# One decoder layer on one core: the output projection in a written TensorE order, logit constants by one product, and shortened hops in the routing chain

## The chip, the cores and the metric

The kernel runs on one core of a Trainium2 chip. A core has a matrix engine (TensorE; PE in the profile, its weight loads PEld), a vector engine (DVE), a scalar engine (ACT), a fourth engine (GpSimd; POOL) and a fifth that mostly issues DMAs (SyncE; SP). Each runs its own list of instructions in order; they wait for one another by semaphores. The metric is the device time of one execution in microseconds, less being better. Three executions of the kernel before took 1434.85, 1434.45 and 1433.2 us, with a median of 1434.45 us.

## The reference

One decoder layer on x of 1024 rows by 1024 columns, in float32. What matters here is its second half:

```python
# o: the merged result of two attention branches, 1024x1024
h = layer_norm(ALPHA * x + o @ w_out, ln1_g, ln1_b)
g_logits = h @ w_grp + b_grp             # 4 groups
g_sel = argmax(g_logits)                 # one group for each row
e_logits = (h @ w_rtr + b_rtr)[g_sel]    # 8 experts in that group
top_l, top_i = top_k(e_logits, 2)
weight = softmax(g_logits)[g_sel] * softmax(top_l)
# each row goes to its two experts of 32:
# y = (silu(h @ w_gate[e]) * (h @ w_up[e])) @ w_down[e]
out = layer_norm(ALPHA * h + sum(weight * y), ln2_g, ln2_b)
```

## The kernel before

The program has these stages, one after another: the input projections, the two attention branches, the merge of the branches (products of L711), the output projection with layer norm and routing, the 32 experts, and the last layer norm. The change touches the output projection, the routing and the first experts; the lists of all engines are the same up to there.

**Output projection.** The 1024 rows are worked in 8 tiles of 128 rows (the loop over `i`). A tile is 48 products of 128x512 (L982): 8 slices `k` of the inner dimension, three terms each (high by high, high by low and low by high halves of split operands), and two halves of the columns. The last tile does all products of its first half before those of its second. DVE then drains the sum into `wr` (L985, with ALPHA·x added), takes mean and variance (L987, L792, L794, with a power on POOL, L795) and applies the layer norm in two operations: L799 (minus the mean, times the gain) and L800 (times 1/deviation, plus the bias). TensorE transposes the normalised rows (L490, 8 squares), ACT copies them to `hT` (L1001), and 8 products `hT` by `wrt` (L956, two instructions each) give 36 router logits for each row; DVE adds the router bias `brt` (L963). SP writes the rows to `h_d` (which the experts gather from) and to `acc_d` (which they add to).

**Constants of this stage.** `gb1` (gain and bias of the layer norm, L828 and L829), `wrt` (router weights, L831), `brt` (L833) and `cons` (a table of small constants, L835) are loaded by SP, in this order. `prefetch` (L752) loads expert weights of 1 MB each into a ring of slots as these come free; SP issues these on the same queue.

**Routing.** `route` works a group of tiles at once, groups (0,1), (2,3,4), (5,6) and (7). DVE finds the best group and the two best experts (`first_max`, L858 to L865), makes the 0/1 matrix `am` (L888) and running counts `ac` (L898); TensorE turns these into places (`pp`, L899 and L900); DVE builds `at_place` (L922) and TensorE turns values into lists for each expert (`ft`, L923). The last group ends with `tkv` (L926, L927), the rows and weights of each expert. POOL scatters the same into `tab` (`store`, L938); the last groups' scatters (`late`) stand after the first gathers. Then experts that got over 128 rows are counted (L1017 to L1031, `novi`).

**Experts.** For each expert POOL gathers its rows from `h_d` (L1049, needs `tkv` and the written `h_d`), TensorE transposes them (`turn`, L1066), ACT and DVE split them (L59, L60) and the weights (`parts`, L1076, L1077) into high and low halves, TensorE multiplies (`up` L1089, `down` L1112), and POOL adds the result to `acc_d` (L1117). An expert's 3 MB of weights free their slots as they are split, and the next loads start from that.

**What sets the order.** Tiles of shared memory come from pools with few buffers (`s` three, `pt` one, `pv` one). In the output projection a scheduler that simulates the program places the instructions of all engines; `tc.issue_after` holds single pieces back. In the experts the order of TensorE is that of the code.

## Time and profile before

| what | value |
| --- | --- |
| median of three runs | 1434.45 us |
| profiled execution | 1431.84 us |
| its span | 1430.1 us |
| TensorE busy | 1331.9 us, 93% of the span |
| DVE busy | 1114.9 us, 78% |
| ACT busy | 764.4 us, 53% |
| POOL busy | 460.3 us, 32% |
| mean granted TensorE clock | 0.968 of full speed |

The profiled execution has 1.7 us outside of its span, and it is 2.6 us below the median of the three runs. Times in the rows are microseconds from the start of the span. TensorE is busy nearly everywhere, so the places that matter are those where it is not: in 40 slices of 36 us each, only the slice from 1037 us on (6 tenths) and the last two are below 8 tenths. The output projection runs from 921 us to 1030 us, the routing of the last tiles up to 1048 us, and the experts from 1053 us to 1387 us.

### The profile page before, as it was taken

How to read it: one execution, taken by the hardware profiler on the slowest of the kernel's cores; microseconds unless marked ns; L12 is line 12 of the kernel's file. 1: busy time of each engine (PE TensorE's matmuls, PEld its weight loads, DVE VectorE, ACT ScalarE, POOL GpSimd, SP SyncE). 2: the span in 40 equal slices, each digit the busy share in tenths (PEclk: the TensorE clock that was granted, in tenths of full speed). 3: DMA queues.
4: the chain of work that ended last, by engine and by line, in shares of the span. 5: the costliest groups of instructions: out<-in, count | busy, mean ns of one | idle time of the engine just before them, and what ended most of it. 6: DMA issues, size and time to landing. Idle time of an engine off the chain costs nothing. (4 is left out here: it accounts for less than half of the span.)

```text
span 1430.1 us, 20066 instructions
## 1 busy us (share of the span) xinstructions
PE 1331.9 (93%) x6779; PEld 1100.2 (77%) x6795; DVE 1114.9 (78%) x2273; ACT 764.4 (53%) x1378; POOL 460.3 (32%) x463
## 2 busy tenths in 40 slices
PE   8999999999999999999999999999969999998960
PEld 7878888878887787888878778888757778776640
DVE  5323699889997787888889965655869999998856
ACT  4323323221116788888879731211238888886744
POOL 1112323222223335453444100001334454443326
PEclk9999999999998999999999999999969999999985
DMA  6023334498333232732521264664659999999936
GB/s 234 16 74 133 111 116 149 152 279 285 138 106 112 67 107 90 195 105 82 152 74 38 97 264 160 253 237 154 230 186 329 344 325 317 317 329 329 320 74 235
DMA packets 69477, 261.36 MB, mean 183 GB/s; under 512 B 15092, under 2 KB 16974, under 8 KB 57085
## 3 DMA queue, kind: packets, MB, share of 16 engines
q1 hardware_dynamic: 59644, 243.24, 49.3%
q0 software_dynamic: 9728, 16.82, 5.1%
q8 instruction: 54, 0.88, 0.3%
q14 instruction: 51, 0.41, 0.1%
HBM read 219.19 MB, written 70.70 MB: 203 GB/s over the span
## 5 line engine op out<-in xcount | busy, mean ns | idle before, releaser
L1089 PE MATMUL pt<-slot,slot 128*128 128x512 f32 x768 | 199.9, 407 | 10.3 <-DVE slot L1077 4.9
L1077 DVE TENSOR_TENSOR slot<-slot,slot 128x1024 fp32r<-128x1024 f32 x160 | 191.3, 1219 | 15.8 <-ACT slot L1076 11.7
L1076 ACT CAST slot<-slot 128x1024 fp32r<-128x1024 f32 x160 | 165.8, 1048 | 36.9 <-PE pt L1089 25.9
L1089 PEld LDWEIGHTS pt<-slot,slot 128*128 128x128 f32 x768 | 142.1, 192 | 49.7 <-DVE slot L1077 8.9
L186 POOL TENSOR_TENSOR wl<-wr,wh 128x1024 fp32r<-128x1024 f32 x39 | 94.9, 2434 | 264.5 <-ACT wh L185 256.0
L324 DVE TENSOR_SCALAR_CACHE_REDUCE jk<-idx,cand 128x384 bf16<-128x384 f32 (+1 forms) x186 | 164.4, 942 | 1.2
L60 DVE TENSOR_TENSOR ptl<-pt,pth 128x512 fp32r<-128x512 f32 (+1 forms) x240 | 148.5, 638 | 18.5 <-ACT pth L59 17.5
L204 PE MATMUL s<-xh,wh 128*128 128x512 f32 x496 | 154.9, 393 | 2.4 <-DVE wi L168 1.4
L204 PE MATMUL s<-xh,wl 128*128 128x512 f32 x496 | 154.5, 391 | 0.0
L204 PE MATMUL s<-xl,wh 128*128 128x512 f32 x496 | 154.4, 391 | 0.0
L59 ACT CAST pth<-pt 128x512 fp32r<-128x512 f32 (+1 forms) x240 | 127.8, 548 | 45.4 <-PE pt L490 38.6
L465 POOL TENSOR_SCALAR pb<-pb,st 128x128 f32<-128x128 f32 (+3 forms) x120 | 91.7, 783 | 183.1 <-ACT pth L59 55.5
L185 ACT CAST wh<-wr 128x1024 fp32r<-128x1024 f32 x39 | 41.0, 1051 | 190.9 <-PE s L204 92.2
L1117 POOL DMA_INDIRECT acc_d<-wr,tkv x32 | 76.8, 2400 | 138.7 <-DVE wr L1116 132.5
L204 PEld LDWEIGHTS s<-xh,wh 128*128 128x128 f32 x496 | 92.5, 188 | 22.9 <-issue 2.6
L204 PEld LDWEIGHTS s<-xl,wh 128*128 128x128 f32 x496 | 93.6, 189 | 19.5
L204 PEld LDWEIGHTS s<-xh,wl 128*128 128x128 f32 x496 | 93.4, 189 | 19.3
L484 ACT ACTIVATE pb<-pb,st 128x128 f32<-128x128 f32 (+7 forms) x128 | 99.6, 779 | 15.5 <-DVE st L482 14.4
L1112 PE MATMUL s<-slot,hT 128*128 128x512 f32 x384 | 100.7, 408 | 2.0 <-DVE hT L60 1.5
L982 PE MATMUL s<-slot,slot 128*128 128x512 f32 x384 | 93.5, 398 | 0.0
L1112 PEld LDWEIGHTS s<-slot,hT 128*128 128x128 f32 x384 | 70.6, 191 | 26.8 <-DVE hT L60 11.2
L490 PE MATMUL pt<-ident,pb 128*128 128x128 f32 x576 | 90.5, 276 | 0.7 <-DVE ptl L60 0.4
(340 smaller groups left out, 2918.8 us busy)
## 6 DMA issues: line engine op xcount, KB each, us to landing
slot<-in_w_ex_dram SPq DMA_DIRECT2D x80, 1024.0 KB
wr<-in_w_tt_dram SPq DMA_DIRECT2D x31, 512.0 KB
ring<-in_w_ex_dram SPq DMA_DIRECT2D x11, 1024.0 KB
b_d<-r_d SPq DMA_DIRECT2D x16, 576.0 KB
xw<-in_xw_dram SPq DMA_DIRECT2D x8, 718.0 KB
last<-in_w_ex_dram SPq DMA_DIRECT2D x5, 1024.0 KB
z_ga<-sh SPq DMA_DIRECT2D x8, 512.0 KB
slot<-b_d SPq DMA_DIRECT2D x8, 512.0 KB
```

The lines of the kernel that those rows point to most:

```text
L59: S.copy(h, src)
L60: V.tensor_tensor(l, src, f(h), op=ALU.subtract)
L186: G.tensor_tensor(wl, wr, f(wh), op=ALU.subtract)
L204: PE.matmul(z[:, c], w[:, k * P:(k + 1) * P], xx[:, k, c], start=(k == 0 and w is wh and xx is xh), stop=(k == KD - 1 and w is wl))
L324: V.tensor_scalar(jk[:, :n], idx[:, OFF[i]:OFF[i] + n], t, None, op0=op, op1=ALU.add, accum_out=cnt[:, i - 2:i - 1])
L465: G.tensor_scalar(ap, ap, s, 1.0, op0=ALU.mult, op1=ALU.mult)
L484: S.activation(p, p, AF.Exp, bias=st[:, 0, j:j + 1], scale=-1.0, accum_out=st[:, 1, j:j + 1])
L982: mm = PE.matmul(s[:, HALF[c]], MS[i][:, a, k], WO[k][:, b, HALF[c]], start=(k == 0 and x == 0), stop=(k == KD - 1 and x == 2)).ins
L1076: S.copy(w[:, 0], self.w[k2 // 4][:, k2 % 4 // 2])
L1077: d = V.tensor_tensor(w[:, 1], self.w[k2 // 4][:, k2 % 4 // 2], f(w[:, 0]), op=ALU.subtract).ins
L1089: PE.matmul(self.a, self.xt[:, a, k * P:(k + 1) * P], w[:, b, (k - k2) * 512:(k - k2 + 1) * 512], start=(k == 0 and x == 0), stop=(k == KD ...
L1112: PE.matmul(s[:, c], self.hT[:, a, k * P:(k + 1) * P], w[:, b, c], start=(k == 0 and x == 0), stop=(k == 1 and x == 2))
```

## The change

**Order of the output projection.** The scheduler no longer places TensorE's instructions there. The products are a generator that stops after each slice `k`, and a table (`hook`) says what stands between: transposes of the tile before, its logits, and pieces of the routing. The other engines are still placed by the scheduler.

**Logits.** The rows are transposed before the layer norm. The gain is multiplied into `wrt` once, and a logit is then (1/deviation) · (row · (gain·W) − mean · sum(gain·W)) + (sum(bias·W) + router bias). The two sums (`nu` and `vb`) come from DVE products and sums over `wrt` and `cons` (which now also holds gain and bias, in 16 more columns) and from one product of TensorE with a matrix of ones (`logit_constants`, L944), which stands in tile 0 behind 7 of its 8 slices. The router bias is loaded behind `cons`, into `vb`.

**Routing.** The groups are (0,1), (2,3), (4,5), (6) and (7); `route` is a generator in three pieces (up to the counts, up to `at_place`, the rest), and the pieces of the earlier groups are called from the table. In the last chain products that nobody uses (`keep_warm`, 14, 4 and 16 of 128x512) stand between the hops.

**The last tile.** The layer norm's second operation on it (`shift`) is issued in two halves: one after its logits, one after the first piece of its routing; the write to `h_d` follows. Its first half is transposed and multiplied with the router before the products of its second half are all done.

**First experts.** Expert 0's rows are split in two halves and its products go in another order of terms. The count of overfull experts (18 small operations of DVE) moves behind expert 0's split, and the load of `novi` on SP moves behind four weight loads. The scatters of groups (4,5), (6) and (7) into `tab` (8 instead of 2) stand behind expert 3's gather on POOL. The descriptor memory goes from 8192 to 4096.

```diff
+            for x in HALF if self.n == 0 else (slice(0, T),):
+                self.split = split(self.xt[:, 0, x], self.xt[:, 1, x], s[:, x])
...
+            terms = list(enumerate(((0, 0), (1, 0), (0, 1)) if self.n else ((0, 0), (0, 1), (1, 0))))
+            for k, (x, (a, b)) in ([(k, t) for t in terms for k in (k2, k2 + 1)] if self.n == 0 else
+                                   [(k, t) for k in (k2, k2 + 1) for t in terms]):
...
-        brt = wo.tile([P, 36], F32, name="brt")
-        nc.sync.dma_start(brt, A["b_rt"].partition_broadcast(P))
-        cons = wo.tile([P, 328], F32, name="cons")
+        cons = wo.tile([P, 344], F32, name="cons")
         nc.sync.dma_start(cons, A["cons"])
+
+        nu, vb = wo.tile([P, 36], F32, name="nu"), wo.tile([P, 36], F32, name="vb")
+        nc.sync.dma_start(vb, A["b_rt"].partition_broadcast(P))
+        ones_f, gsum = wo.tile([P, P], F32, name="ones_f"), wo.tile([P, 2, 36], F32, name="gsum")
+        bw = wo.tile([P, KD, 36], F32, name="bw")
+        G.memset(ones_f, 1.0)
+        V.tensor_tensor(bw, wrt, cons[:, 336:344, None].to_broadcast([P, KD, 36]), op=ALU.mult)
+        V.tensor_tensor(wrt, wrt, cons[:, 328:336, None].to_broadcast([P, KD, 36]), op=ALU.mult)
+        for x, w in enumerate((wrt, bw)):
+            V.tensor_reduce(gsum[:, x], w.rearrange("p k e -> p e k"), axis=X, op=ALU.add)
+
+        def logit_constants():
+            t = ps.tile([P, 512], F32, name="pv")
+            PE.matmul(t[:, 0:72], ones_f, gsum.rearrange("p x e -> p (x e)"), start=True, stop=True)
+            V.tensor_scalar(nu, t[:, 0:36], -1.0, None, op0=ALU.mult)
+            V.tensor_tensor(vb, vb, t[:, 36:72], op=ALU.add)
...
+            for j in range(B):
+                d = V.tensor_tensor(ac[:, i0 + j + 1], ac[:, i0 + j], am[:, j], op=ALU.add).ins
+            yield d
             pp = ps.tile([P, 512], F32, name="pv")[:, 0:32 * B].rearrange("p (b e) -> p b e", b=B)
             for j in range(B):
-                V.tensor_tensor(ac[:, i0 + j + 1], ac[:, i0 + j], am[:, j], op=ALU.add)
                 PE.matmul(pp[:, j], tri, am[:, j], start=True, stop=False)
                 PE.matmul(pp[:, j], ones_b[:, 0:P], ac[:, i0 + j], start=False, stop=True)
...
+            at_places = []
+            for j in range(B):
+                for x in range(2):
+                    at_places.append(wo2.tile([P, P], F32, name="at_place", bufs=4))
+                    V.tensor_scalar(at_places[-1], places, sf[:, 0, j, x:x + 1], None, op0=ALU.is_equal)
+            yield
...
-            if i0 + B < NT:
+            if i0 + B < 5:
...
-            if last:
-                with tc.issue_after(mm):
-                    logits(hT, lt, range(KD))
-                held = gather(i - 1, lt)
...
-                    done = scale(xr[:, cc], gb1[:, :, cc], mv, rs)
...
-            if i != NT - 2:
-                logits(hT, lt, range(KD))
-            nc.sync.dma_start(h_d[ts], xr)
-            kept.append(nc.sync.dma_start(acc_d[ts], xr).ins)
-            if last:
-                with tc.issue_after(done):
-                    route(*held)
-            if i != NT - 2:
-                g = gather(i, lt)
-                if g:
-                    route(*g)
...
+        GROUPS = {1: (0, 2), 3: (2, 2), 5: (4, 2), 6: (6, 1), 7: (7, 1)}
...
+        def turn_rows(i, c):
+            if c == 0:
+                hT = wo2.tile([P, T], F32, name="hT", bufs=1)
+                rows[i] += (hT, ps.tile([P, 512], F32, name="pt"))
+            xr, hT = rows[i][0], rows[i][2]
+            t = transposed([xr[:, k * P:(k + 1) * P] for k in range(4 * c, 4 * c + 4)])
+            S.copy(hT[:, HALF[c]], t)
...
+            V.scalar_tensor_tensor(xr, xr, mv[:, 0:1], gb1[:, 0], op0=ALU.subtract, op1=ALU.mult)
+            if i < NT - 1:
+                shift(i, slice(0, D))
+
+        def shift(i, cc):
+            xr, ts, rs = rows[i][0], slice(i * P, (i + 1) * P), rows[i][5]
+            V.scalar_tensor_tensor(xr[:, cc], xr[:, cc], rs, gb1[:, 1, cc], op0=ALU.mult, op1=ALU.add)
+            if cc.stop == D:
+                nc.sync.dma_start(h_d[ts], xr)
+                kept.append(nc.sync.dma_start(acc_d[ts], xr).ins)
...
+            o = lgs[e][:, i - i0]
+            V.scalar_tensor_tensor(o, nu, mv[:, 0:1], lt[:, 0:36], op0=ALU.mult, op1=ALU.add)
+            d = V.scalar_tensor_tensor(o, o, rs, vb, op0=ALU.mult, op1=ALU.add).ins
+            if i == NT - 1:
+                with tc.issue_after(d):
+                    shift(i, HALF[0])
+            if i == e:
+                routes[e] = route(i0, lgs[e], B)
+                d = next(routes[e])
+            if i == NT - 1:
+                with tc.issue_after(d):
+                    shift(i, HALF[1])
...
+        def hook(i, at):
+            if i == NT - 1:
+                at = {3: (0, 1), 7: (2,), 9: (3,), 11: (5,), 12: (4,), 14: (6,)}.get(at, ())
+            else:
+                at = {0: (7,), 1: (0, 1), 3: (2,), 5: (3,)}.get(at, ())
+            for x in at:
+                if x < 2 and i > 0:
+                    turn_rows(i - 1, x)
+                    if x:
+                        norm(i - 1)
+                elif x == 2 and i > 0:
+                    logits(i - 1, 0)
+                    logits(i - 1, 1)
+                elif x in (3, 4) and i - 2 in routes:
+                    next(routes[i - 2])
+                elif x == 7 and i - 3 in routes:
+                    next(routes[i - 3])
+                elif x == 5:
+                    turn_rows(i, 0)
+                elif x == 6:
+                    logits(i, 0)
...
+        def keep_warm(n):
+            t = ps.tile([P, 512], F32, name="s")
+            for x in range(n):
+                PE.matmul(t, ident_b, ones_b[:, 0:512], start=(x == 0), stop=(x == n - 1))
+        with tc.manual_schedule(engines={mybir.EngineType.PE}):
+            for i in range(NT):
+                for at, _ in enumerate(products(i)):
+                    hook(i, at)
+                    if i == 0 and at == 6:
+                        logit_constants()
+                prefetch({0: 6, 2: 1, 4: 1, 6: 1, 7: 5}.get(i, 0))
+            last = NT - 1
+            next(routes[6])
+            turn_rows(last, 1)
+            norm(last)
+            logits(last, 1)
+            next(routes[6])
+            keep_warm(14)
+            next(routes[7])
+            keep_warm(4)
+            next(routes[7])
+            ex = {e: make(e) for e in range(2)}
+            for e in range(2):
+                ex[e].fetch()
+            overflow = ps.tile([P, 512], F32, name="pv")[:, 0:32]
+            PE.matmul(overflow, ones_b[:, 0:P], ac[:, NT], start=True, stop=True)
+            keep_warm(16)
...
+    def count_overflow():
...
+        V.tensor_copy(novi, novf)
...
-    with tc.issue_after(ex[1].fetched):
-        late[0]()
...
+            if e == 2:
+                with tc.issue_after(ex[3].fetched):
+                    for store in late:
+                        store()
+            with tc.issue_after(last_place[0]) if e == 0 else nullcontext():
+                ex[e].up(0)
+                ex[e].up(2)
+                if e > 0:
+                    ex[e - 1].flip()
+                if e == 0:
+                    with tc.issue_after(ex[0].split):
+                        count_overflow()
...
-    nc = bacc.Bacc("TRN2", target_bir_lowering=False, num_devices=1, dynamic_dma_scratch_size=8192)
+    nc = bacc.Bacc("TRN2", target_bir_lowering=False, num_devices=1, dynamic_dma_scratch_size=4096)
```

TensorE at the end of tile 0, before. `slot_9420` to `slot_9455` are the split output weights of the 8 slices, `slot_8976` and `slot_9479` the split rows of tiles 0 and 1.

```order
L982 MATMUL s<-slot_9440,slot_8976 128x512 x6
L982 MATMUL s<-slot_9445,slot_8976 128x512 x6
L982 MATMUL s<-slot_9450,slot_8976 128x512 x6
L982 MATMUL s<-slot_9455,slot_8976 128x512 x6
L982 MATMUL s<-slot_9420,slot_9479 128x512 x6
L982 MATMUL s<-slot_9425,slot_9479 128x512 x6
```

The same place now (L1087 is the product that was L982).

```order
L1087 MATMUL s<-slot_9440,slot_8976 128x512 x6
L1087 MATMUL s<-slot_9445,slot_8976 128x512 x6
L1087 MATMUL s<-slot_9450,slot_8976 128x512 x6
L944 MATMUL pv<-gsum,ones_f 128x72
L1087 MATMUL s<-slot_9455,slot_8976 128x512 x6
L1087 MATMUL s<-slot_9420,slot_9493 128x512 x6
L1087 MATMUL s<-slot_9425,slot_9493 128x512 x6
L490 MATMUL pt<-ident,wr 128x128 x8
```

The product of the constants stands between the seventh and the eighth slice of tile 0, and tile 0's transposes follow two slices into tile 1.

DVE around tile 0, before: the split of tile 1's rows, the drain of tile 0 (L985) and its layer norm.

```order
L60 TENSOR_TENSOR slot_9479<-slot_8863,slot_9479 128x1024
L985 SCALAR_TENSOR_TENSOR wr<-wr,s 128x1024
L60 TENSOR_TENSOR slot_9581<-slot_8864,slot_9581 128x1024
L987 BN_STATS bs<-wr 128x6 x2
L792 BN_AGGR mv<-bs 128x2
L794 TENSOR_SCALAR rs<-mv 128x1
L799 SCALAR_TENSOR_TENSOR wr<-wr,mv,gb_9458 128x1024
L800 SCALAR_TENSOR_TENSOR wr<-wr,rs,gb_9458 128x1024
L838 CAST tri<-cons 128x128
L841 CAST vali<-cons 128x8 x2
```

The same stretch now: what makes `gsum` (L937 to L940, with casts of other constants between) and what reads the constants' product stands ahead of the drain (L1092).

```order
L60 TENSOR_TENSOR slot_9493<-slot_8863,slot_9493 128x1024
L937 TENSOR_TENSOR bw<-wrt,cons 128x288
L950 CAST tri<-cons 128x128
L953 CAST vali<-cons 128x8 x2
L1200 COPY pid<-cons 128x1
L938 TENSOR_TENSOR wrt<-wrt,cons 128x288
L940 TENSOR_REDUCE gsum<-bw 128x36
L940 TENSOR_REDUCE gsum<-wrt 128x36
L945 TENSOR_SCALAR nu<-pv 128x36
L946 TENSOR_TENSOR vb<-vb,pv 128x36
L1092 SCALAR_TENSOR_TENSOR wr<-wr,s 128x1024
```

The first operation of DVE that reads `cons` stood behind tile 0's layer norm and stands now ahead of its drain.

TensorE behind the last products of the projection, before: logits of tile 6, transposes and logits of tile 7, then the places of the last groups.

```order
L982 MATMUL s<-slot_9455,slot_10234 128x512 x3
L956 MATMUL pt<-wrt,hT 128x36 x8
L923 MATMUL pv<-val,at_place 128x64 x2
L490 MATMUL pt<-ident,wr 128x128 x8
L956 MATMUL pt<-wrt,hT 128x36 x8
L899 LDWEIGHTS tri
L899 MATMUL pv<-am,tri 128x32
```

The same place now.

```order
L1087 MATMUL s<-slot_9455,slot_10190 128x512 x3
L1013 LDWEIGHTS tri
L1013 MATMUL pv<-am,tri 128x32
L1014 LDWEIGHTS ones_b
L1014 MATMUL pv<-ac,ones_b 128x32
L490 MATMUL pt<-ident,wr 128x128 x4
L1123 MATMUL pt<-wrt,hT 128x36 x4
L1041 MATMUL pv<-val,at_place 128x64 x2
L1173 LDWEIGHTS ident_b
L1173 MATMUL s<-ones_b,ident_b 128x512
```

Behind the last product stand now half of the transposes and half of the logits that stood there, and tile 6's logits stand ahead of it.

## Rows read from the trace of the kernel before

**Rows 1.** The page's line of busy time, share of the span and instructions by engine.
```profile
PE 1331.9 (93%) x6779; PEld 1100.2 (77%) x6795; DVE 1114.9 (78%) x2273; ACT 764.4 (53%) x1378; POOL 460.3 (32%) x463
```

**Rows 2.** Busy time (and instructions) by engine in stretches, granted clock, DMA share, GB/s.
```profile
920.90:1029.60 108.70, 108.70 (x566) 90.70 (x565) 67.45 (x167) 18.88 (x29) 21.30 (x19) 1.00 0.57 210
1029.60:1053.40 23.80, 11.23 (x62) 9.84 (x61) 19.39 (x112) 1.99 (x6) 10.02 (x12) 0.61 0.68 253
1053.40:1062.30 8.90, 7.28 (x20) 5.40 (x21) 2.07 (x2) 2.06 (x2) 4.75 (x5) 0.52 0.52 174
1062.30:1070.00 7.70, 7.70 (x44) 6.54 (x43) 5.35 (x6) 6.68 (x8) 0.00 (x0) 1.00 0.64 203
1100.00:1200.00 100.00, 100.00 (x477) 79.62 (x476) 98.04 (x105) 84.77 (x104) 46.68 (x32) 1.00 0.96 330
```

**Rows 3.** Timeline of TensorE at tiles 0 and 1: start, duration, operation, count.
```profile
920.91 23.59 PE L982 MATMUL s<-slot,slot 128*128 128x512 f32 x101
944.34 1.03 PE L490 MATMUL pt<-ident,wr 128*128 128x128 f32 x8
...
949.84 1.87 PE L956 MATMUL pt<-wrt,hT 128*128 128x36 f32 x16
951.54 2.11 PE L982 MATMUL s<-slot,slot 128*128 128x512 f32 x8
```

**Rows 4.** Timeline of SP's loads and DVE at tile 0; in brackets idle time and releaser.
```profile
924.20 0.43 SPq L829 DMA_DIRECT2D gb<-in_ln_b_dram  x1
...
926.70 0.33 SPq L835 DMA_DIRECT2D cons<-in_cons_dram  x1
...
938.88 1.28 DVE L800 SCALAR_TENSOR_TENSOR wr<-wr,rs,gb 128x1024 f32<-128x1024 f32 x1 [1.08 <-DMA gb<-in_ln_b_dram]
940.08 0.22 DVE L838 CAST tri<-cons 128x128 bf16<-128x128 f32 x1
```

**Rows 5.** Timeline from the last product to the first gather.
```profile
1026.31 9.47 SPq L752 DMA_DIRECT2D slot<-in_w_ex_dram  x5
...
1028.59 0.95 PE L982 MATMUL s<-slot,slot 128*128 128x512 f32 x3
...
1029.57 0.69 DVE L985 SCALAR_TENSOR_TENSOR wr<-wr,s 128x512 f32<-128x512 f32 x1 [0.36 <-PE s L982]
...
1034.11 0.75 DVE L800 SCALAR_TENSOR_TENSOR wr<-wr,rs,gb 128x512 f32<-128x512 f32 x1
1034.23 0.58 ACT L1001 COPY hT<-pt 128x512 f32<-128x512 f32 x1 [7.04 <-PE pt L490]
...
1035.89 3.47 PE L956 MATMUL pt<-wrt,hT 128*128 128x36 f32 x16
...
1039.39 0.19 DVE L963 TENSOR_TENSOR lg<-pt,brt 128x36 f32<-128x36 f32 x1 [0.41 <-PE pt L956]
...
1040.24 0.15 DVE L858 TENSOR_REDUCE fm<-lg 128x1 f32<-128x4 f32 x1
...
1045.21 0.20 DVE L888 TENSOR_TENSOR am<-one,o 128x32 bf16<-128x32 f32 x1
...
1048.24 0.18 DVE L927 TENSOR_TENSOR tkv<-pv,found 128x32 f32<-128x32 f32 x1
...
1049.13 1.05 POOL L1049 DMA_INDIRECT wr<-h_d,tkv  x1 [1.69 <-issue]
```

**Rows 6.** Timeline of TensorE at experts 0 and 1.
```profile
1053.45 1.97 PE L1066 MATMUL s<-ident,wr 128*128 128x128 f32 x8 [4.76 <-DMA wr<-h_d,tkv]
1057.78 4.71 PE L1089 MATMUL pt<-slot,slot 128*128 128x512 f32 x11 [0.47 <-DVE slot L60]
1062.32 1.04 PE L1066 MATMUL s<-ident,wr 128*128 128x128 f32 x8
```

**Rows 7.** Timeline of TensorE: transposes of two later experts.
```profile
1291.74 1.04 PE L1066 MATMUL s<-ident,xg 128*128 128x128 f32 x8
1303.86 1.04 PE L1066 MATMUL s<-ident,xg 128*128 128x128 f32 x8
```

More of the change, by code (lines that the diff above doesn't have):

```diff
@@ L846, in layer_kernel @@
                                   oob[:, None, :].to_broadcast([P, NT, NE * 2])).ins
-        scatters, late, kept = [], [], []
+        scatters, late, kept, last_place = [], [], [], []
         places, ids = cons[:, 192:320], cons[:, 320:328]
@@ L950, in route, with products @@
                 late.append(store)
-        group, lg = [], None
-        def logits(hT, lt, ks):
-            for k in ks:
-                PE.matmul(lt[:, 0:36], hT[:, k * P:(k + 1) * P], wrt[:, k], start=(k == 0), stop=(k == KD - 1))
-        def gather(i, lt):
-            nonlocal group, lg
-            if not group:
-                group = [n for n in ((0, 1), (2, 3, 4), (5, 6), (7,)) if i in n][0]
-                lg = wo2.tile([P, len(group), 36], F32, name="lg")
-            V.tensor_tensor(lg[:, i - group[0]], lt[:, 0:36], brt, op=ALU.add)
-            if i == group[-1]:
-                done, group = group, []
-                return done[0], lg, len(done)
-        for i in range(NT):
-            ts = slice(i * P, (i + 1) * P)
+            yield
+        GROUPS = {1: (0, 2), 3: (2, 2), 5: (4, 2), 6: (6, 1), 7: (7, 1)}
+        rows, lgs, routes = {}, {}, {}
+        def products(i):
             s = ps.tile([P, T], F32, name="s")
-            last = i == NT - 1
+            xr = rp.tile([P, D], F32, name="wr", bufs=3)
+            nc.sync.dma_start(xr, A["x"][i * P:(i + 1) * P])
+            bs = wo2.tile([P, 2, 6], F32, name="bs")
+            rows[i] = xr, bs
             if i + 1 < NT:
@@ L987, in layer_kernel @@
                     V.bn_stats(bs[:, c], xr[:, HALF[c]])
-            mv, rs = moments(bs, wo2, 2)
-            if last:
-                with tc.issue_after(mm):
-                    logits(hT, lt, range(KD))
-                held = gather(i - 1, lt)
-            hT = wo2.tile([P, T], F32, name="hT", bufs=1)
-            lt = ps.tile([P, 512], F32, name="pt")
-            for cs in ((0,), (1,)) if last else ((0, 1),):
-                cc = slice(512 * cs[0], 512 * cs[-1] + 512)
-                with tc.issue_after(done) if cs == (1,) else nullcontext():
-                    done = scale(xr[:, cc], gb1[:, :, cc], mv, rs)
-                for c in cs:
-                    t = transposed([xr[:, k * P:(k + 1) * P] for k in range(4 * c, 4 * c + 4)])
-                    S.copy(hT[:, HALF[c]], t)
@@ new lines, in logits @@
+        def logits(i, c):
+            hT, lt = rows[i][2:4]
+            for k in range(4 * c, 4 * c + 4):
+                PE.matmul(lt[:, 0:36], hT[:, k * P:(k + 1) * P], wrt[:, k], start=(k == 0), stop=(k == KD - 1))
+            if c == 0:
+                return
+            lt, mv, rs = rows[i][3:6]
+            e = next(e for e in GROUPS if i <= e)
+            i0, B = GROUPS[e]
+            if i == i0:
+                lgs[e] = wo2.tile([P, B, 36], F32, name="lg")
+            o = lgs[e][:, i - i0]
[10 more added lines that the diff above has]
+                    shift(i, HALF[1])
@@ L1128, in make @@
-    def make(e):
-        return Expert(e, tkv[:, TURN[e], 0:1], tkv.bitcast(F32)[:, TURN[e], 1:2], None)
-    ex = {e: make(e) for e in range(2)}
-    V.tensor_copy(novi, novf)
-    for k2 in (0, 2):
-        ex[0].parts(k2)
-    for e in range(2):
-        ex[e].fetch()
+    with tc.issue_after(last_place[0]):
+        for k2 in (0, 2):
+            ex[0].parts(k2)
     prefetch(1)
-    with tc.issue_after(ex[1].fetched):
-        late[0]()
     with tc.manual_schedule(engines={mybir.EngineType.PE}):
```

219 lines of the change are left out of this document (108 added, 111 removed).

## Prediction

> **What bounds the kernel now.** I read the busy line of the page first: TensorE is busy 93% of the span [rows 1], so what it idles, or does more slowly, is what a change can win or lose. The stretches by stage come next [rows 2]. [...]
>
> Then the timelines. 101 products take 23.59 us, 0.2336 each [rows 3]. What the change needs early are constants, so I looked for when they come [rows 4]: the layer norm's bias, issued at 924.20, releases L800 at 938.88, 14.7 us later. `cons` is issued behind it, at 926.70. Its first reader starts at 940.08 without a wait of its own: `cons` has come by then, and on one queue, behind the bias, hardly before 938.88.
>
> **The change part by part.**
>
> *The constants' product, L944.* It stands behind 42 products: 920.91 + 42 x 0.2336 = 930.7. It needs `gsum`, whose first operation (L937) needs `cons`: between 938.88 and 940.08, I take 939.4. That the router bias no longer stands ahead of `cons` moves its issue by some 1.5 us, but the landing of the bias before it shows that the loads ahead decide, not the issue. Four operations over 288 elements a partition (L937, L938, two L940) have no row of their own; a cast of 128 elements takes 0.22 [rows 4] and one with 512 elements 0.75 [rows 5], so 0.22 to 0.75 each, I take 0.4, with 0.3 for the small casts between: 1.9 us (1.2 to 3.3). L944 starts at 941.3: a stall of 10.6 us (9.4 to 12.7). Queued behind it on TensorE are 6 products of tile 0 and all of tiles 1 to 7, 342 in all; tile 0's drain on DVE stands behind the same constants. Tiles 1 to 7 keep TensorE full, so nothing later takes the wait up: **+10.6**.
>
> *The clock after the stall.* TensorE ran at 0.61 and 0.52 where it had pauses of a few us, and took 7.28 us of work at half speed before the clock came back at 1062.3 [rows 2]. After 10.6 idle us I expect the same. At half the clock a product takes twice 0.2336. If it lasts as long as in the row, 8.9 us, half of it is lost, 4.5 us; if the clock does not fall, 0. I take the middle: **+2.2**.
>
> *More work ahead of the last product.* The logits of tile 6 (1.70, 949.84 to 951.54 [rows 3]) and half of tile 7's (0.85) now stand ahead, also half of tile 7's transposes (half of 1.03 less overlap, 0.4) and some five small products (L944, places, lists) at 0.12, as a logits instruction, to 0.23, as a wide product, 1.05 together with their loads: **+4.0**. The transposes of tiles 0 to 6 stand two slices (12 products, 2.8 us) behind the tile's last product, and these hide the drain (the half drain takes 0.69, starting 0.03 behind the last end [rows 5], a whole one about 1.3). If a split of the next rows stands before it on DVE this cover is just gone, some 0.1 to 0.5 per tile, up to 3 us; with DVE at 62% I take 0.
>
> *The chain behind the last product* [rows 5, 6]. Before, with 0 at the end of the last product (1029.54): logits of tile 7 are added by 1039.58 (10.0), its routing runs from 1040.24 to 1048.42 (18.9), the gather is issued at 1049.13 (19.6), transposes start at 1053.45 (23.9), expert 1's transposes at 1062.32 (32.8). In this, tile 6's logits, the whole layer norm (0.75 per half operation) and full transposes and logits (3.47 at half clock) stood ahead of tile 7's logits. After: half drain 0.7, four transposes 0.6, copy 0.6 (L1001), 8 instructions of logits at 1.87/16 each 0.9, two small DVE operations, with the hand-overs between: 4.5. The routing took 8.2 with another group's beside it; alone I take 7.6, so `tkv` at 12.1 and the gather at 12.8, as 0.7 lay between before. But the gather also needs `h_d`. Its write waits for the second half of the shift, behind the routing's first piece (1040.24 to 1045.41, 5.2) and its own 0.75: 4.5 + 5.2 + 0.75 = 10.4. How long 512 KB take to land has no row of its own; the gather's 4.3 is the nearest, so 14.7, and with four weight loads of 1 MB ahead of it up to 17. At the other end it hides completely (12.8). I take 13.5. Transposes then at 17.8. Before, 4.3 us passed from transposes to the second product, half of it because of the clock; with the split in halves and a warm engine I take 1.9, and 12 products at 0.2336, 2.8: expert 1's transposes at 22.5. Gain 32.8 - 22.5 = **-10.3** (7 if `h_d` is late or the unused products do not hold the clock, 13 if `h_d` hides and the routing takes 7).
>
> *The count of overfull experts.* Its DVE operations stood in the gather's shadow (18 at 0.15 to 0.20 as the small ones in [rows 5], some 3.4 us). Now they stand between expert 0's and 1's splits. Just there DVE is busy 5.35 of 7.70, a little later 98.04 of 100.00 [rows 2], so part of it shows: **+0.7** (0 to 2.7).
>
> *At nothing:* the eight late scatters (POOL is busy 46.68 of 100.00 in the experts), the smaller descriptor memory, the load of `novi` and the groups. Their cover is POOL's and SP's slack; without it, a gather of expert 4 that is late by 8 x 1.05 us (as the gather at 1049.13) would cost at most a few us, as gathers run ahead by an expert. The experts themselves are a rigid tail: paced by TensorE (100.00 of 100.00 busy [rows 2]) and later by weights (12.12 us between the transposes of two experts from 1291.74 on [rows 7]); their loads start from the release of expert 0's slots, which moves with the stage.
>
> *Sum against the profiled execution:* 4.0 + 10.6 + 2.2 - 10.3 + 0.7 = +7.2; 1431.84 + 7.2 = 1439.0. The median shown is 2.6 above that execution: 1434.45 + 7.2 = 1441.7 us.
>
> The rows show 14.7 us from issue to use for the bias, with the queue full of 1 MB loads [rows 4]. [...]
>
> Of passing a waiting instruction: TensorE's pauses before L1066 [rows 6] are no proof, as nothing behind them was free. [...] No row of this case decides it.
>
> **The rivals.**
>
> 1. *No stall, so faster.* The constants come in time: `cons` is landed by 929 since its place in the queue is another, or TensorE passes the wait. Then 4.0 - 10.3 + 0.7 = -5.6, 1428.9. For it: its issue is earlier by a place. Against it: the bias, issued earlier still, came at 938.88. It decides from a stall under about 3 us, that is a landing before 932.
> 2. *The chain hardly gets shorter.* `h_d` comes late (behind four loads) and the clock falls in spite of the unused products, so the gain is 5: +12.5, 1447. For it: 0.61 and 0.52 in this stretch, and five loads taking SP 9.47 us from 1026.31 on. Against it: four transposes and half the logits less on the chain are sure.
> 3. *The tail takes the shift up.* If the weights, and not the release of slots, set the end, a shift of the stage hardly shows: 1434.5. For it: the weight-bound pace of 12.12. Against it: the ring has the same number of slots, full before expert 0 in both, so its loads start at expert 0's release.
>
> **How the numbers follow.** Forecast (slower by the stall) 0.76, rival 1 0.08, rival 2 0.09, rival 3 0.07. The terms' own ends give 1434.45 + (3.3 + 9.4 + 0 - 13 + 0) = 1434.2 and, with 4.0 + 12.7 + 4.5 - 7 + 2.7, 1451; not all fall together, so the likeliest case's own range is 1437.5 to 1446, and the range for 8 in 10 is 1434.0 to 1448.0, which takes in rivals 2 and 3 and leaves out rival 1. About 0.2% (2.9 us) is what a measurement of this kernel can tell from no change, so same is 1431.6 to 1437.3: faster 0.08 (rival 1), same 0.13 (rival 3 and the forecast's low end), slower 0.79.
>
> **What would show it.** In the profile after: a gap of TensorE before L944 of about 10 us, released by DVE `gsum`, which itself waited for the DMA of `cons`; a granted clock under 1 just behind; the last product at about 1046; expert 0's transposes about 18 us later, at a clock near 1; and the distance from there to the end as before. The prediction is wrong if L944 has no gap, if the chain gains over 13 us, or if the experts end at the time of before in spite of a later start.

## The result and the profile after

The changed kernel took 1445.24 us in the median of 4 runs (1442.51 to 1448.97), the kernel before 1433.83 us beside it: a ratio of 1.008, with a 95% interval of 1.006 to 1.010, so 8.6 to 14.3 us slower. Forecast were 1441.7 us, +7.2. The four times lie in two pairs, near 1442.5 and near 1448.4; the profiled execution belongs to the lower pair. Its span is 1440.7 us, 10.6 above that of before.

TensorE at tile 0 after the change; columns as in [rows 3], with idle time and releaser in brackets:

```profile
919.96 9.87 PE L1087 MATMUL s<-slot,slot 128*128 128x512 f32 x42
940.26 0.67 PE L944 MATMUL pv<-gsum,ones_f 128*128 128x72 f32 x2 [10.43 <-issue]
940.68 6.66 PE L1087 MATMUL s<-slot,slot 128*128 128x512 f32 x18
947.18 1.03 PE L490 MATMUL pt<-ident,wr 128*128 128x128 f32 x8
```

The 42 products are followed by a gap of 10.43 us before L944. The 18 products behind it take 6.66 us, where the same 18 take 4.39 in e1 below, and 4.39 in e8 at a granted clock of 1.00. What the gap waits for shows on SP and DVE:

```profile
923.25 0.43 SPq L926 DMA_DIRECT2D gb<-in_ln_b_dram  x1
...
924.20 0.43 SPq L930 DMA_DIRECT2D cons<-in_cons_dram  x1
...
937.89 0.46 DVE L937 TENSOR_TENSOR bw<-wrt,cons 128x288 f32<-128x288 f32 x1 [13.51 <-DMA cons<-in_cons_dram]
...
939.53 0.63 DVE L940 TENSOR_REDUCE gsum<-wrt 128x36 f32<-128x288 f32 x1
```

`cons` releases DVE 13.7 us after its issue, and DVE itself had idled 13.51 us for it: the load that stood in [rows 4] without a waiting reader has one now. L944 names no engine as its releaser, but `gsum` ends at 940.16, 0.1 us before it.

The chain behind the last product (its end is 1045.70), which answers to [rows 5, 6]:

```profile
1044.76 0.94 PE L1087 MATMUL s<-slot,slot 128*128 128x512 f32 x3
...
1047.81 1.79 PE L1123 MATMUL pt<-wrt,hT 128*128 128x36 f32 x8 [0.67 <-ACT hT L1103]
...
1056.33 0.33 SPq L1117 DMA_DIRECT2D h_d<-wr  x1
...
1058.25 0.18 DVE L1045 TENSOR_TENSOR tkv<-pv,found 128x32 f32<-128x32 f32 x1
...
1058.53 3.61 PE L1173 MATMUL s<-ones_b,ident_b 128*128 128x512 bf16 x16
1058.83 0.33 SPq L752 DMA_DIRECT2D last<-in_w_ex_dram  x1
1059.83 1.84 POOL L833 DMA_INDIRECT wr<-h_d,tkv  x1 [10.35 <-DVE slot L862]
1060.72 16.10 SPq L752 DMA_DIRECT2D slot<-in_w_ex_dram  x2
...
1068.51 1.97 PE L850 MATMUL s<-ident,wr 128*128 128x128 f32 x8 [6.37 <-DMA wr<-h_d,tkv]
1071.15 4.93 PE L875 MATMUL pt<-slot,slot 128*128 128x512 f32 x12 [0.68 <-ACT slot L59]
1075.92 1.03 PE L850 MATMUL s<-ident,wr 128*128 128x128 f32 x8
```

The gather is issued 3.50 us behind the write of `h_d`. Its row names an operation of DVE as the releaser; but in all ten profiles of the experiments below this distance is 3.50 to 3.52 us too, while that from the end of `tkv` varies from 0.9 to 1.4, and in e1, e4 and e5 the row names `h_d` (e5's stand there). So it is the landing of `h_d` that starts the gather.

From the gather's issue to the first transpose 8.7 us pass, where it was 4.3 [rows 5, 6]. Two weight loads of 1 MB are issued beside it, one 1.0 us before and one 0.9 us behind (the other of its row comes at 1076.5). In the trace's packets those of the two loads run from 1059.9 to 1067.6, and those of the gather begin only at 1065.1. Before the change the same two loads came 3.2 and 13.6 us behind the gather's issue:

```profile
1052.30 0.34 SPq L752 DMA_DIRECT2D last<-in_w_ex_dram  x1
...
1062.70 12.71 SPq L752 DMA_DIRECT2D slot<-in_w_ex_dram  x4
```

What SP had waited for between 1035 and 1080 (us in total, times, longest), the rows of these loads and of `novi`, first before and then after the change:

```profile
SPq L1164 <- DVE novi L1132: 14.4, 1, 14.4
SPq L752 <- DVE slot L1077: 16.2, 3, 10.0
```

```profile
SPq L752 <- PE pv L1196: 1.6, 1, 1.6
SPq L752 <- DVE slot L862: 1.5, 1, 1.5
```

Before, SP was held at the load of `novi` (L1164) until 1051.3, and then 10.0 us more by a weight split of expert 0 that ended at 1062.67. Now the first load is released by the product right behind `tkv` (L1196), and the second by a split of expert 0's weights (L862), which run from 1058.35 on.

The granted clock shows how TensorE went through this (columns as in [rows 2]):

```profile
930.30:940.20 9.90, 0.00 (x0) 0.00 (x0) 2.27 (x8) 0.00 (x0) 0.00 (x0) 0.58 1.02 362
940.20:945.60 5.40, 5.34 (x14) 4.31 (x15) 2.27 (x4) 1.04 (x1) 0.00 (x0) 0.50 0.01 5
1047.90:1054.80 6.90, 6.68 (x22) 4.06 (x24) 5.43 (x29) 0.41 (x2) 1.48 (x1) 0.51 0.65 273
1054.80:1065.00 10.20, 6.11 (x31) 2.66 (x29) 6.68 (x24) 0.00 (x0) 4.59 (x4) 1.00 0.77 259
1065.00:1075.30 10.30, 6.12 (x18) 4.89 (x19) 1.91 (x6) 2.22 (x3) 8.13 (x9) 0.50 0.37 133
```

In the gap nothing ran on TensorE, with the DMA engines full (a share of 1.02). The clock fell to half three times: in the gap (0.50 from about 932 to 945.6), at 1047.9 (0.51 up to 1054.8), and during the wait for the gather (0.50 from 1065.0 to 1075.3); with the unused products it was full only between 1054.8 and 1065.0 (1.00), and expert 0 ran at half clock again (0.50).

Against the start of the projection (before: 920.91, after: 919.96) the last product ends 17.1 us later than before, expert 1's transposes come 14.6 us later, and the end is 11.6 us later.

### The profile page after: what moved, and what is told of

It is laid out like the page before. It is cut to its first block, busy times and chain, and to the rows that moved or that the text cites. A ratio compares the mean times of both kernels' runs of the same rounds, so it can differ in the third digit from the quotient of the medians.

```text
span 1440.7 us, 20186 instructions
## 1 busy us (share of the span) xinstructions
PE 1337.3 (93%) x6814; PEld 1100.0 (76%) x6831; DVE 1122.8 (78%) x2323; ACT 764.5 (53%) x1381; POOL 459.9 (32%) x464
## 5 line engine op out<-in xcount | busy, mean ns | idle before, releaser
L875 PE MATMUL pt<-slot,slot 128*128 128x512 f32 x768 | 196.9, 403 | 8.0 <-DVE slot L862 3.8
L862 DVE TENSOR_TENSOR slot<-slot,slot 128x1024 fp32r<-128x1024 f32 x160 | 191.5, 1220 | 10.3 <-ACT slot L861 5.8
L204 PE MATMUL s<-xh,wl 128*128 128x512 f32 x496 | 154.9, 392 | 0.0
L1087 PE MATMUL s<-slot,slot 128*128 128x512 f32 x384 | 96.9, 406 | 0.0
```

The costliest lines, as they stand in the source:

```text
L204: PE.matmul(z[:, c], w[:, k * P:(k + 1) * P], xx[:, k, c], start=(k == 0 and w is wh and xx is xh), stop=(k == KD - 1 and w is wl))
L862: d = V.tensor_tensor(w[:, 1], self.w[k2 // 4][:, k2 % 4 // 2], f(w[:, 0]), op=ALU.subtract).ins
L875: PE.matmul(self.a, self.xt[:, a, k * P:(k + 1) * P], w[:, b, (k - k2) * 512:(k - k2 + 1) * 512], start=(k == 0 and x == 0), stop=(k == KD ...
L1087: PE.matmul(s[:, HALF[c]], MS[i][:, a, k], WO[k][:, b, HALF[c]], start=(k == 0 and x == 0), stop=(k == KD - 1 and x == 2))
```

## The experiments

Since the stages ahead of the projection move between executions (its first product starts between 917.9 and 923.9), chains are compared from that product. The tail is the distance from expert 1's transposes to the end of the span. Profiles are of one execution, times are medians of several; the ratio is to the kernel before as it ran beside each version (medians of 1431.94 to 1433.83 us):

| kernel | last product's end | expert 1's transposes | between them | tail | time, median | ratio to before (95%) |
| --- | --- | --- | --- | --- | --- | --- |
| before | 108.6 | 141.4 | 32.8 | 367.8 | 1433.83 | |
| changed | 125.7 | 156.0 | 30.2 | 364.8 | 1445.24 | 1.008 (1.006 to 1.010) |
| e1 constants first | 114.8 | 144.5 | 29.7 | 366.3 | 1435.96 | 1.0012 (1.0000 to 1.0024) |
| e2 loads after gather | 125.6 | 152.3 | 26.7 | 369.3 | 1443.41 | 1.0069 (1.0051 to 1.0086) |
| e3 both | 115.0 | 141.2 | 26.1 | 368.1 | 1434.56 | 0.9999 (0.9982 to 1.0015) |
| e4 both, no unused products | 116.4 | 141.6 | 25.2 | 369.1 | 1432.92 | 0.9999 (0.9983 to 1.0015) |
| e5 all constants in time | 112.6 | 137.9 | 25.3 | 368.0 | 1429.91 | 0.9981 (0.9968 to 0.9995) |
| e6 product later | 113.1 | 141.8 | 28.7 | 370.3 | 1435.07 | 1.0015 (0.9999 to 1.0032) |
| e7 fewer weight loads | 125.7 | 154.9 | 29.2 | 355.2 | 1432.48 | 1.0006 (0.9995 to 1.0017) |
| e8 products in the pauses | 112.6 | 135.4 | 22.8 | 367.3 | 1426.88 | 0.9964 (0.9949 to 0.9979) |
| e9 as e8, loads beside the gather | 112.6 | 141.6 | 29.1 | 369.5 | 1430.67 | 0.9993 (0.9979 to 1.0006) |
| e8 again | 112.6 | 135.3 | 22.7 | 367.0 | 1425.42 | 0.9956 (0.9943 to 0.9969) |

**e1. The constants ahead of the weight loads.**

```diff
-        nc.sync.dma_start(cons, A["cons"])
+        cons_load = nc.sync.dma_start(cons, A["cons"]).ins
...
-                prefetch({0: 6, 2: 1, 4: 1, 6: 1, 7: 5}.get(i, 0))
+                with tc.issue_after(cons_load) if i == 0 else nullcontext():
+                    prefetch({0: 6, 2: 1, 4: 1, 6: 1, 7: 5}.get(i, 0))
```

> The changed kernel with one edit: SP issues the gain, bias, router weights and constants ahead of the five 1 MB weight loads of the output projection, and not behind them. Theory (the stall is a wait for constants that queue behind 5 MB): they come some 5 us after their issue, the gap of 10.4 us before the constants' product and the 2.3 us at half clock behind it go, and the span falls by about 12.7 us, from 1440.7 to 1428, below the kernel before (1430.1). Rival A (TensorE would wait there anyway, for a drain or for split rows): the gap keeps more than 5 us, span above 1435. Rival B (the weight loads, now some 8 us later, are late for something in the stage): the gap goes, but the span falls by less than 8 us.

The gap fell to 2.0 us, and the products behind it took the 4.39 us that they take in e8 at a granted clock of 1.00:

```profile
934.61 0.41 PE L944 MATMUL pv<-gsum,ones_f 128*128 128x72 f32 x2 [2.00 <-issue]
934.83 4.39 PE L1087 MATMUL s<-slot,slot 128*128 128x512 f32 x18
```

The last product ends 10.9 us earlier than in the changed kernel, and the median is 9.3 us lower. The theory holds for the gap; 2.0 us of it are left, as gain and bias (1 MB) still went ahead (without them ahead, in e5, no gap is left). The span fell by 7.2 us and not by 12.7, under the 8 us of rival B, but the projection started 2.8 us later in this execution; from its first product to the end 10.0 us are gone, so rival B is not seen. The kernel was not below that of before: the stall was most of the loss, not all.

**e2. The loads behind the gather.**

```diff
+            if n in (17, 18):
+                tc.add_manual_dep(d, ex[0].fetched.name, sync, reason="after expert 0 has its rows")
```

> The changed kernel with one edit: the two weight loads that are issued beside the first gather wait until expert 0's rows have come. Theory (the gather queues behind 2 MB of weights): the distance from the gather's issue to the first transpose falls from 8.7 us to about 4.3 as before the change; the transposes then begin while the clock is still full, and from the gather's issue to expert 1's transposes 16.1 us become about 9, so the span falls by some 7 us, to 1434. Rival A (the gather waits for the write of the last rows, issued 3.5 us ahead of it): the distance stays above 8 us and nothing changes. Rival B (the two loads are then late for later experts): the chain falls by 7 us and the span by less than 3.

```profile
1059.73 1.85 POOL L835 DMA_INDIRECT wr<-h_d,tkv  x1 [10.43 <-DVE slot L864]
...
1064.84 1.97 PE L852 MATMUL s<-ident,wr 128*128 128x128 f32 x8 [2.80 <-DMA wr<-h_d,tkv]
```

Gather to transposes fell from 8.7 to 5.1 us, with the write of `h_d` 3.5 us ahead of the gather's issue as in the changed kernel: the loads were the cause of the longer transfer (rival A falls). Of what is left over 4.3, POOL's issue is 0.8 (1.85 against 1.05 before the change). But the transposes still took 1.97 us, as before the change at a granted 0.52 [rows 2, 6] (1.09 in e8 at 1.00), so the chain won 3.5 us and not 7. The median is 1.8 us lower, with overlapping spreads (1441.65 to 1444.39, in the changed kernel 1442.51 to 1448.97), so no gain in time is shown by this run alone.

**e3. Both.** The two edits together.

> Both edits, constants first and the two loads after the gather. If the two costs are separate places on one path: 12.7 + 7 = 20 us less than the changed kernel, a span of about 1421, 9 us below the kernel before. Rival (the weight loads set the end, and what is won ahead of the experts is lost in waits for weights behind expert 24): a span of 1425 or more with both gaps gone.

The last product as in e1, the chain as in e2: they add up on the chain (14.8 us less at expert 1 than the changed kernel). The median is 10.7 us below the changed kernel and not 20; of the two sizes in the expectation, the 12.7 was 10.9 and the 7 was 3.5. The span of 1432.6 us meets the number of the rival, but not its cause: of the 14.8 us on the chain 3.4 are taken by a later start of the projection and 3.3 by a tail of 368.1 us, which is that of the kernel before (367.8). The chain to expert 1 is now as long as before the change (141.2 against 141.4), and so is the time.

**e4. Without the unused products.**

```diff
-            keep_warm(14)
...
-            keep_warm(4)
...
-            keep_warm(16)
```

> Both edits, and the 34 unused products of the routing chain left out. Theory (they bring the clock back to full at 1054.8 and hold it until the gather has landed): without them TensorE is at half clock from the last products to expert 1, the first 12 products and 8 transposes take some 4 us more, and the last hops of the routing about 1 us more: 5 us above the kernel with both edits. Rival (the pauses between the hops let the clock fall anyway, or the chain is not TensorE's): within 1.5 us of it.

```profile
1040.30:1057.60 17.30, 3.82 (x27) 3.02 (x24) 14.11 (x59) 0.99 (x3) 5.48 (x4) 0.64 0.65 249
1057.60:1065.50 7.90, 7.22 (x20) 5.61 (x21) 4.14 (x12) 2.22 (x3) 6.21 (x7) 0.50 0.83 306
```

The rival holds: the chain takes 25.2 us against 26.1 with them, and the median is 1.6 us lower, each within the other's spread. Where they stood they brought nothing.

**e5. The constants ahead of gain and bias too** (on e4).

```diff
-        gb1 = wo.tile([P, 2, D], F32, name="gb1")
-        nc.sync.dma_start(gb1[:, 0], A["ln1_g"].partition_broadcast(P))
-        nc.sync.dma_start(gb1[:, 1], A["ln1_b"].partition_broadcast(P))
         wrt = wo.tile([P, KD, 36], F32, name="wrt")
         nc.sync.dma_start(wrt, A["w_rt"])
         cons = wo.tile([P, 344], F32, name="cons")
-        cons_load = nc.sync.dma_start(cons, A["cons"]).ins
+        nc.sync.dma_start(cons, A["cons"])
+        gb1 = wo.tile([P, 2, D], F32, name="gb1")
+        nc.sync.dma_start(gb1[:, 0], A["ln1_g"].partition_broadcast(P))
+        cons_load = nc.sync.dma_start(gb1[:, 1], A["ln1_b"].partition_broadcast(P)).ins
```

> As the kernel with both edits and no unused products, and in addition the router weights and the constants are loaded ahead of the layer norm's gain and bias (1 MB less in front of them). Theory (what remains of the stall, 2.0 us, and of the half clock behind it, 1.4 us, is the landing of the constants behind gain and bias): the gap before the constants' product falls under 0.5 us, the products behind it run at full clock, and the time falls by 3 us, to 1430, some 3.5 us below the kernel before. Rival (the weight stream sets the end and keeps its place): the gap goes, the time stays within 1 us of 1433.

```profile
921.23 0.42 SPq L929 DMA_DIRECT2D cons<-in_cons_dram  x1
...
923.71 0.46 DVE L939 TENSOR_TENSOR bw<-wrt,cons 128x288 f32<-128x288 f32 x1 [1.35 <-DMA cons<-in_cons_dram]
...
927.64 0.34 PE L946 MATMUL pv<-gsum,ones_f 128*128 128x72 f32 x2
927.78 4.39 PE L1089 MATMUL s<-slot,slot 128*128 128x512 f32 x18
...
1039.99 0.33 SPq L1119 DMA_DIRECT2D h_d<-wr  x1
...
1043.49 1.18 POOL L835 DMA_INDIRECT wr<-h_d,tkv  x1 [9.21 <-DMA h_d<-wr]
```

No gap is left: with only the router weights ahead of it in this stage, `cons` releases its reader 2.5 us after its issue, where it took 13.7. The last product ends 3.8 us earlier than in e4. The median is 3.0 lower, as expected (2.6 by the ratios, whose intervals overlap), and the kernel is now faster than before, if by only 0.2%. Its projection is 3.9 us longer than that of before (112.6 against 108.6): the added work, with no stall in it.

**e6. The product later, the loads as they were.** Tile 0's logits go with it, and DVE's readers of the constants stand behind tile 0's drain (of the edit, only the lines for TensorE are shown).

```diff
-                elif x == 2 and i > 0:
+                elif x == 2 and i > 1:
...
-                    if i == 0 and at == 6:
+                    if i == 1 and at == 5:
                         logit_constants()
+                        logits(0, 0)
+                        logits(0, 1)
```

> The changed kernel with the loads in their old order, but the constants' product moved from tile 0 to behind the sixth slice of tile 1, with tile 0's logits behind it, and the operations of DVE that read the constants placed behind tile 0's drain. Theory (the place of the waiting instruction in TensorE's list is what costs, as all behind it waits): TensorE comes there at 940.4, the constants' sums are ready at about 942.5, the gap falls from 10.4 to about 2 us, and the span by some 10 us, as in the kernel with the constants first. Rival (the stall moves to something else, as tile 0's transposes behind the drain): a gap of more than 5 us remains somewhere in tiles 0 and 1.

```profile
938.75 0.41 PE L946 MATMUL pv<-gsum,ones_f 128*128 128x72 f32 x2 [0.28 <-issue]
```

The gap is 0.28 us, with the same loads in the same order, and the last product ends 12.6 us earlier than in the changed kernel. So it took two things to make the stall: constants that land late (e1, e5), and their readers placed ahead of work that was ready. Undoing either one removes it. TensorE did not pass the waiting product: in the changed kernel it ran nothing in 9.90 us, with 42 products ahead of L944 and ready ones behind it (in e6, with nothing that waits between them, the first 60 run in 14.02 us).

**e7. Fewer weight loads.** Experts 18 to 23 use the weights that are still in their slots, 18 of 96 loads are left out.

```diff
+            if 54 <= n < 72:
+                weights.append(weights[n - 18])
+                loads.append(loads[n - 18])
+                continue
```

> The changed kernel, in which experts 18 to 23 use the weights that are in their slots, so that 18 of 96 weight loads are left out (its output is not the reference's). Theory (TensorE's waits behind expert 24 are for the weight stream, 77 loads that run without a pause from the release by expert 0 to the end): the five longer distances between transposes (10.9 to 12.9 us) become 9.65 as the others, 11 us less, and the last stage perhaps 2 us less: a span of about 1428. Rival (they are waits for gathers on POOL or for the scatter-adds): at least three of the longer distances stay, and the span is above 1436.

Transposes of experts 26 to 28 in the changed kernel, then of experts 26 to 28 in this one:

```profile
1315.66 1.04 PE L850 MATMUL s<-ident,xg 128*128 128x128 f32 x8
...
1328.51 1.04 PE L850 MATMUL s<-ident,xg 128*128 128x128 f32 x8
...
1339.41 1.04 PE L850 MATMUL s<-ident,xg 128*128 128x128 f32 x8
```

```profile
1314.95 1.04 PE L854 MATMUL s<-ident,xg 128*128 128x128 f32 x8
1324.61 1.04 PE L854 MATMUL s<-ident,xg 128*128 128x128 f32 x8
1334.26 1.04 PE L854 MATMUL s<-ident,xg 128*128 128x128 f32 x8
```

All distances are 9.65 us now, where 12.85 and 10.90 stood, and expert 31's transposes come at 1363.19, not 1373.59. The span is 1430.1 us (1428 was expected), the tail 9.6 us shorter. So TensorE is full from the ring's stock up to expert 26, and behind that the weight stream decides. That stream starts at expert 0's release, so a shift of the stage should stay a shift at the end. The table agrees: in the executions with all loads, expert 1's transposes lie 20.7 us apart (135.3 to 156.0), but the tails only 5.5 us (364.8 to 370.3), and the late ones are not all short (369.3 us in e2). Whether time won inside the later experts would be lost again is not shown; no run changes their pace with all loads in place.

**e8. The unused products in the pauses** (on e5).

```diff
             next(routes[6])
+            keep_warm(4)
             turn_rows(last, 1)
             norm(last)
+            keep_warm(3)
             logits(last, 1)
             next(routes[6])
-            keep_warm(14)
+            keep_warm(20)
             next(routes[7])
-            keep_warm(4)
+            keep_warm(6)
...
-            keep_warm(16)
+            keep_warm(26)
```

> As the kernel with all constants in time, but with unused products again, now also in the pauses right behind the last product (4 and 3) and more of them behind the later hops (20, 6) and in the wait for the gather (26). Theory (the clock is granted by how busy TensorE is, and before they stood behind the pauses in which it fell): the clock stays at 1.00 from the projection to expert 1, the 12 products of expert 0 take 2.9 us and not 5.4, and the distance from the last product to expert 1's transposes falls from 25 to about 21 us. Rival A (the clock falls all the same at some point, as in the changed kernel): above 24. Rival B (it holds, but the time stays within 1.5 us of the kernel without them, since the weight stream sets the end).

```profile
919.50:1032.10 112.60, 112.60 (x605) 94.60 (x605) 79.22 (x252) 20.06 (x34) 19.46 (x20) 1.00 0.58 213
1032.10:1050.30 18.20, 15.66 (x84) 7.72 (x82) 14.19 (x59) 0.99 (x3) 6.12 (x5) 1.00 0.60 231
1050.30:1055.00 4.70, 4.02 (x21) 3.20 (x22) 1.98 (x6) 2.22 (x3) 3.82 (x5) 1.00 0.83 288
```

The clock stays at 1.00 through the whole chain, with TensorE busy 15.66 of 18.20 us where e4 had 3.82 of 17.30 and a clock of 0.64; how the clock is granted beyond these numbers is not shown. Expert 0's 12 products take 3.06 us (5.24 in e5), and the chain is 22.8 us. The median is 3.0 us below e5's (the intervals of the ratios overlap; e8 again is 4.5 below it); this is the fastest version, below both kernels. The edit raises the number of unused products from the 34 of the changed kernel to 59 and moves 7 of them into the earlier pauses; no run does only one of the two, so their shares are not told apart.

**e9 and e8 again.** The hold of the two loads taken out of e8, and e8 beside it.

> As the kernel with the unused products in the pauses, but the two weight loads are no longer held until expert 0's rows have come: they are issued beside the gather again, as in the changed kernel. Theory (the gather queues behind 2 MB of weights): the distance from the gather's issue to the first transpose grows from 5.2 to about 8.7 us, the clock falls in the longer wait, and expert 1's transposes come 4 to 8 us later against the start of the projection; as the weight stream behind expert 0 moves with them, the time grows by 2 to 5 us, to about 1430. Rival (what the chain loses the earlier loads give back, so that holding them brought nothing): the chain is longer and the time within 1 us of 1426.9.

> The kernel with the unused products in the pauses once more, beside the kernel whose loads are not held, on the same chip: about 1427, some 5.5 us below the kernel before; the clock stays at 1.00 from the projection to expert 24.

Gather and first transposes, in e9 and then in e8 again:

```profile
1047.52 1.84 POOL L833 DMA_INDIRECT wr<-h_d,tkv  x1 [9.20 <-DVE slot L862]
...
1056.17 1.61 PE L850 MATMUL s<-ident,wr 128*128 128x128 f32 x8 [4.19 <-DMA wr<-h_d,tkv]
```

```profile
1046.94 1.85 POOL L835 DMA_INDIRECT wr<-h_d,tkv  x1 [9.21 <-DVE slot L864]
...
1051.97 1.09 PE L852 MATMUL s<-ident,wr 128*128 128x128 f32 x8 [0.56 <-DMA wr<-h_d,tkv]
```

Without the hold the gather takes 8.65 us again (5.03 in e8 beside it), TensorE is slower behind the wait (expert 0's transposes take 1.61 us against 1.09 beside it, its 12 products 5.31 against 3.06, and 5.47 in e4 at a granted 0.50), the chain is 6.4 us longer and the median 5.2 us higher than e8's beside it. In a chain that is otherwise clean the collision costs nearly its full price; whether the earlier loads give back the 1 us between the two is within the spread of the times.

## Why the prediction was right, and where it was not

*The stall.* Right in place, cause and size: 10.6 forecast, 10.43 measured. e1 (all but 2.0 us) and e5 remove it by the loads, e6 by the place; they take back 10.9, 13.2 and 12.6 us at the last product. That the products behind L944 would wait with it was the author's assumption, for which no row of before stands; the 9.90 us without an instruction of TensorE show it. That the size is so close is partly luck: `cons` released its reader at 937.89 and not at 939.4, but TensorE stood ready 0.9 us earlier than reckoned, and the operations up to `gsum` took 2.3 us and not 1.9; these differences nearly cancel.

*The clock behind it.* Forecast 2.2; 6.66 instead of 4.39 us is 2.3. The forecast was the middle between no loss and 4.5, so this hit is partly luck too.

*More work ahead of the last product.* Forecast 4.0; with no stall (e5, e8) the projection is 3.9 us longer than before, with TensorE busy in all of its 112.60 us (e8), so what was added showed in full. Costing the drains at nothing held: no gap stands before the transposes of tiles 0 to 6.

*The chain behind the last product.* This is the step that failed: 10.3 forecast as gain, 2.6 measured (32.8 to 30.2). Up to `tkv` it went as worked out (12.7 us against 12.1, `h_d` issued at 10.6 against 10.4). Of the 7.7 us that are missing, 0.6 are the gather's issue (14.1 against 13.5), 4.4 the gather itself, and 2.7 the stretch from expert 0's transposes to expert 1's (7.4 against 4.7).

The gather's issue waited for `h_d`, as the prediction feared, but this cost little: 3.5 us from the write's issue, some 0.7 us behind what `tkv` would have allowed (12.7, and the 0.7 that lay between them before). The transfer itself was put at the 4.3 us of before; it took 8.7, since two 1 MB loads were now set free just there: the first as SP no longer stands at the load of `novi`, the second by expert 0's weight splits, which now run right behind `tkv`. (Why the second waited for a later split before the change, though three ran early there, is not shown.) I had put the load of `novi` among the edits at nothing, and priced no transfer for the splits, though before the first load's packets began only at 1053.3, when the gather was nearly done. That the loads made the gather longer is shown by e2 and e9, with 3.6 us each (8.7 to 5.1, and 8.65 against 5.03). Packets of both run side by side only from 1065.1 to 1067.6: beside the loads the gather's first packet came 5.2 us after its issue, before the change, with no load's packets yet, 1.7 us after it (POOL's issue itself takes 0.8 us longer now).

The other large term is the clock: "a warm engine" was taken from the presence of the unused products, not from what they fill: expert 0 ran at 0.50. It needed both repaired to reach what I had forecast: e8's chain is 22.8 us, against the 22.5 worked out, so the sum was that of a chain without the collision and with a clock that holds.

*The tail.* Forecast +0.7, measured -3.0 (367.8 to 364.8 us from expert 1's transposes to the end) in one pair of executions. Executions of the kernel before spread over 1427.6 to 1438.8, and the tails of the other versions with all loads lie between 366.3 and 370.3, so the cause of the -3.0 stays open; e7 shows that the tail's length hangs on the weight stream (355.2 us with 18 loads less). Around expert 2, where the count stands, 0.36 us more is seen (11.03 against 10.67 between two transposes).

*The time.* That 1445.2 us lies inside the range is in part luck. The chain fell short by 7.7 us, and the tail, for which nothing of the kind was worked out, gave back 3.7 against its forecast; with the tail as forecast the time would have been about 1449, above the 1448.0 of the range. Of the range itself, the upper sum leaves out the up to 3 us that the prediction allowed for drains, and the lower one takes 3.3 for the added work, for which it names no row.

*Rivals.* The first (no stall) fell. The second (chain hardly shorter) came true beside the stall, by loads and clock, but mainly in the gather's transfer and not by a late `h_d`. The third fell in its form: the weight stream sets the end (e7), but it starts with expert 0, and the shift came through.

## What to carry to other kernels

An order written by hand turned one operand's arrival into the business of all that stood behind it on TensorE: with the same loads the gap was 10.43 us at one place of the reader and 0.28 at another (e6). So look up when the constants land (here 13.7 us after their issue, behind what they queue) before placing their first reader, or put the reader late. A transfer on the critical chain is priced with what else is released at that moment: here edits that only moved work past it made it 4.4 us longer. The unused products held the clock where they covered the pauses ahead of the work that profits: the 34 that left pauses open brought nothing here (e4: a chain of 25.2 us without them, 26.1 with them), the 59 that covered them did (e8: a clock of 1.00, a chain of 22.8 us).

## What the runs showed that was not expected

The unused products of the changed kernel were worth nothing (e4 without them is no slower than e3: 1432.92 and 1434.56 us), while 59 of them, some in other places, kept the clock at 1.00 from the projection into the experts (e8). Holding two loads of 1 MB for some 5 us won 3.5 us of the chain in the changed kernel, with no gain in time that stands clear of the spread, but 6.4 us of the chain and 5.2 us of the time in the repaired one. On the chain, the price of one fault depended on the others being gone: only there did the hold also keep the clock up (1.00 in e8; expert 0's transposes take 1.09 us in e8 again and 1.61 in e9, but 1.97 in e2, as at half clock).
